# Modulation products grouped by four beside the long convolutions of a two-layer trunk

## The chip, the cores and the metric

The kernel runs on one core of one Trainium2 chip. Its engines work through queues of their own, in the order of their instructions, and wait for each other by semaphores: TensorE (PE, with its weight loads listed as PEld), VectorE (DVE), ScalarE (ACT), GpSimd (POOL) and SyncE (SP), whose queue issues nearly all the loads and stores of this kernel. The metric is the time of one execution on the device in microseconds (us); lower is better.

## The reference

Two layers of a diffusion trunk run over 1024 latent rows and 128 context rows of width 1024. Each layer first forms a modulation vector from the two condition vectors (one for the latents, one for the context), then mixes the rows by four head groups (latent attention, windowed attention, a gated delta recurrence, a long convolution), and then applies an MLP. The change concerns the first line only:

```python
mod = silu(cond) @ w_ada + b_ada              # w_ada is 1024 x 6144 for each layer
sh1, sc1, gt1, sh2, sc2, gt2 = split(mod, 6)
h = rms_norm(x, g_pre_mix) * (1.0 + sc1) + sh1
o = mixer(h)                  # attention, windowed attention, recurrence, convolution
x = x + gt1 * rms_norm(o, g_post_mix)
h = rms_norm(x, g_pre_mlp) * (1.0 + sc2) + sh2
x = x + gt2 * rms_norm(square(relu(h @ mlp_w1)) @ mlp_w2, g_post_mlp)
```

All inputs are float32. `w_ada` is 24 MB for a layer, read once.

## The kernel before

The Python code is a program of generators. `run_timed` runs several of them side by side in the order of planned times, and a scheduler of the tile framework then sets the order of the instructions on each engine from dependences and its own planned times. What stands in that order is fixed when the program is built; on the chip every engine keeps to it.

The six parts of the modulation are made in three pieces of 2048 columns, by `ada(l, g)` (L385): `g` is 0, 1 or 2. Piece 0 of layer 0 stands at the start of the program (the lead). Three generators run side by side in `layer` (L2134): `rest()` (the projections, then `hyena`, then `attention`), `other()` (the filters and preparation of the recurrence, then `gdn_scan`) and `adas()`, which waits until `rest()` says "proj" and then makes pieces 1 and 2 of its own layer and, in layer 0, piece 0 of layer 1.

In `ada`, the 1024 rows of the weights are eight steps `kt` of 128 rows. In each step four tiles `wada` of 128 x 512 (256 KB) are loaded by SP, and each has one product: the 128 x 32 slice `cst[:, kt]` of the conditions is the stationary side, the weights stream through, and the result is added in the rows 32h to 32h + 31 of one PSUM tile `ada` (h is 0 to 3). So a piece is 32 loads and 32 products, and each product is recorded as two passes (two weight loads and two matmuls). ACT then copies the tile to `adarow`, PE transposes it to `adat`, and DVE adds the bias into `mod`. All `wada` tiles come from the pool "T", which has four buffers, so the fifth load waits for the first product. The pool "L" has eight buffers and holds the weights of the projections. A product stands where the scheduler has put it, alone or beside others.

The names that the steps of the prediction use, in the order of a layer:

- `pj`: the products of the input projections.
- `u`, `dS`, `St`, `sdec`, `sc`, `Q`: the gated delta recurrence, `gdn_scan`. A step reads the state `St` on PE (24 small products `u<-St`), forms `u` on DVE, multiplies on PE again (`dS`, `u<-u`), and DVE updates the state (`St<-sdec,dS`, twice in a step). The next step needs this state. One scan has 16 steps over the latents and 2 over the context.
- `long_conv` runs twice in `hyena`: DVE and POOL make a length-12 transform (`ZA`, `ZB`, `ZC`), PE the forward transforms (`X`), DVE and POOL the products with the filters (`pw`, `Y`; the filter `Hs` is loaded by SP), PE the way back (`iz`), and DVE some 25 additions (`pmx`, `e`, `f`, `y`). At the end DVE multiplies `y` by the rows `x` that SP has loaded from `uscr`.
- `hoT`: the transposes of the convolution's result. `oT`: those of the recurrence's result.
- `S`: the scores of head 0's preparation, with the row maxima `mx` on DVE (`ahead()` in `hyena`, 24 of each). `mT`, `mrow`, `mscr`: the maxima are transposed, written to DRAM and read back as one row of `Q`, after which the first tile `ST` of the attention can run.
- `ST`, `e`, `eh`, `el`, `O`: the attention, one head after another, beside the `S` of the next head.

## Time and profile before

| | us |
|---|---|
| median of 3 runs | 3829.02 |
| the three runs | 3819.71, 3829.02, 3829.53 |
| the profiled execution, its time | 3828.84 |
| the profiled execution, its span | 3827.1 |
| layer 0: last `pj` to first `ST` | 535 to 724 |
| layer 0: attention | 724 to 1020.5 |
| layer 1: last `pj` to first `ST` | 2440 to 2636 |
| layer 1: attention | 2636 to 2902 |

The places of a stage are read from the timeline. A window's row gives the busy time of each engine within it, so that a stretch in which PE is busy nearly all the time can be told from one in which it waits. The granted clock in the same row says at which of its two levels (0.5 is 1.2 GHz, 1.0 is 2.4 GHz) TensorE ran, as a mean over the window.

### The profile page before, as it was taken

The page shows a single profiled execution, that of the slowest core. Times are in us where ns is not written, and L with a number is a line of the kernel's source. Part 1 is how long each engine was busy: PE and PEld are TensorE (multiplying, and loading weights), DVE is VectorE, ACT ScalarE, POOL GpSimd, SP SyncE. Part 2 cuts the span into 40 slices and gives each one's busy share as a digit, 9 for nine tenths or more (in the row PEclk, how much of TensorE's full clock was granted, in tenths as well). Part 3 has the DMA queues.
Part 4 walks back from the last instruction along what each step waited for, and adds up shares of the span by engine and source line. Part 5 has one row for each costly group of instructions (what it writes and reads, how often), then busy time and mean ns, then how long its engine had stood idle before and what let it go on. Part 6 is the DMA issues. An engine that isn't in the chain of part 4 may idle for free. (4 is left out here: it accounts for less than half of the span.)

```text
span 3827.1 us, 57478 instructions
## 1 busy us (share of the span) xinstructions
PE 3531.1 (92%) x21710; PEld 2958.8 (77%) x21710; DVE 2279.6 (60%) x4583; ACT 1355.6 (35%) x2970; POOL 853.1 (22%) x806
## 2 busy tenths in 40 slices
PE   7989888899899999999989798787999999999998
PEld 4879764366689999999968797645666899999997
DVE  5765577696645444444586664768884544444446
ACT  5434343264542222122354234323564422222112
POOL 1151521264430000000131524213553200000003
PEclk9999889897899999999999898897889999999999
DMA  5356486831421111111234465756314211111113
GB/s 202 115 120 158 139 275 202 235 90 39 138 87 47 45 44 34 44 45 45 96 103 131 108 144 161 258 187 177 84 50 138 72 45 45 45 45 42 40 41 121
DMA packets 364672, 405.31 MB, mean 106 GB/s; under 512 B 115815, under 2 KB 237157, under 8 KB 364394
## 3 DMA queue, kind: packets, MB, share of 16 engines
q1 hardware_dynamic: 364394, 401.63, 34.9%
q8 instruction: 171, 2.80, 0.3%
q14 instruction: 107, 0.88, 0.1%
HBM read 298.34 MB, written 103.19 MB: 105 GB/s over the span
## 5 line engine op out<-in xcount | busy, mean ns | idle before, releaser
L213 PE MATMUL hid<-hT,w1h 128*128 128x384 f32 x3072 | 786.5, 335 | 0.1
L213 PE MATMUL pj<-hT,wah 128*128 128x384 f32 x2112 | 575.1, 351 | 9.0 <-ACT wah L253 4.2
L1831 DVE TENSOR_TENSOR acc<-acc,mo 128x512 f32<-128x512 f32 x504 | 346.1, 687 | 391.8 <-PE mo L213 391.8
L213 PEld LDWEIGHTS hid<-hT,w1h 128*128 128x128 f32 x3072 | 557.7, 188 | 14.4 <-ACT h L481 1.1
L213 PE MATMUL hid<-hT,w1l 128*128 128x384 f32 x1536 | 514.1, 335 | 0.0
L213 PE MATMUL mo<-w2h,ul 128*128 128x512 f32 x1116 | 435.0, 392 | 0.0
L213 PE MATMUL mo<-w2h,uh 128*128 128x512 f32 x1080 | 422.7, 391 | 0.0
L213 PE MATMUL mo<-w2l,uh 128*128 128x512 f32 x1080 | 422.7, 391 | 0.0
L213 PEld LDWEIGHTS pj<-hT,wah 128*128 128x128 f32 x2112 | 395.3, 196 | 21.9 <-issue 7.8
L662 POOL TENSOR_TENSOR e<-e,e 128x512 f32<-128x512 f32 (+1 forms) x216 | 307.3, 1424 | 313.8 <-DVE el L232 145.2
L269 POOL TENSOR_TENSOR postr<-postr,mhalf 128x1 f32<-128x1 f32 x36 | 22.3, 621 | 1568.9 <-DVE postr L268 1568.6
L213 PE MATMUL pj<-hT,wal 128*128 128x384 f32 x1056 | 367.5, 348 | 0.7 <-DVE wal L232 0.7
L242 ACT CAST w2h<-w 128x512 fp32r<-128x512 f32 x128 | 70.3, 619 | 732.9 <-PE mo L213 728.8
L213 PEld LDWEIGHTS hid<-hT,w1l 128*128 128x128 f32 x1536 | 288.3, 188 | 2.5
L232 DVE TENSOR_TENSOR el<-e,eh 128x512 fp32r<-128x512 f32 (+1 forms) x252 | 241.4, 977 | 25.1 <-ACT eh L653 20.4
L213 PEld LDWEIGHTS mo<-w2h,ul 128*128 128x128 f32 x1116 | 209.6, 188 | 46.1
L213 PEld LDWEIGHTS mo<-w2h,uh 128*128 128x128 f32 x1080 | 202.8, 188 | 37.5
L213 PEld LDWEIGHTS mo<-w2l,uh 128*128 128x128 f32 x1080 | 202.7, 188 | 36.5
L213 PEld LDWEIGHTS pj<-hT,wal 128*128 128x128 f32 x1056 | 206.3, 195 | 4.6 <-issue 2.0
L1814 DVE SCALAR_TENSOR_TENSOR relu<-hid,relu 128x384 f32<-128x384 f32 x180 | 99.5, 554 | 166.9 <-ACT relu L1813 166.9
L213 PE MATMUL ada<-wada,cst 128*32 128x512 f32 x384 | 130.8, 692 | 45.5 <-DMA wada<-in_w_ada 45.4
L232 DVE TENSOR_TENSOR wal<-wa,wah 128x512 fp32r<-128x512 f32 x88 | 67.6, 773 | 147.2 <-ACT wah L253 118.2
(502 smaller groups left out, 6366.6 us busy)
## 6 DMA issues: line engine op xcount, KB each, us to landing
w<-in_w SPq DMA_DIRECT2D x256, 256.0 KB
wada<-in_w_ada SPq DMA_DIRECT2D x192, 256.0 KB
wa<-in_wa SPq DMA_DIRECT2D x88, 256.0 KB
x<-xres SPq DMA_DIRECT2D x21, 512.0 KB
x<-in_x SPq DMA_DIRECT2D x18, 512.0 KB
Q<-rscr SPq DMA_DIRECT2D x32, 288.0 KB
o<-oscr SPq DMA_DIRECT2D x18, 512.0 KB
xres<-x SPq DMA_DIRECT2D x36, 256.0 KB
```

The lines of the kernel that those rows point to most:

```text
L213: self.last = self.nc.tensor.matmul(out, l, r, start=start, stop=stop, skip_group_check=True)
L232: self.nc.vector.tensor_tensor(out=lo, in0=x, in1=hi.bitcast(F32), op=ALU.subtract)
L242: self.nc.scalar.copy(out=hi[:, q], in_=st)
L269: self.nc.gpsimd.tensor_tensor(out=out, in0=out, in1=self.bcs(self.mhalf[:out.shape[0]], out.shape), op=ALU.pow)
L662: self.nc.gpsimd.tensor_tensor(out=acc, in0=acc, in1=e, op=ALU.add)
L1814: nc.vector.scalar_tensor_tensor(out=r[:, :n], in0=ps[:, :n], scalar=0.0, in1=r[:, :n], op0=ALU.max, op1=ALU.mult)
L1831: nc.vector.tensor_tensor(out=acc[t][:, ns], in0=acc[t][:, ns], in1=ps, op=ALU.add)
```

## The change

`ada` loads the four tiles of a step together and issues their products as a group: the product of h = 3 is placed behind the last product that stood in the program, and the three others behind it. The products of a step are issued when the loads of two later steps have been issued (`len(wait) == 3`), except in the lead, where they follow at once. Two steps in three take their tiles from the pool "L" (eight buffers), the third from "T" (four). `hyena` says "conv" when it has issued its loads, and `adas()` waits for "conv" instead of "proj". In `attention`, `self.heads` is set: from there on all tiles come from "T", and a step's products follow before the loads of the next step. `layer` sets it back.

```diff
--- before.py
+++ after.py
@@ -382,17 +382,37 @@
         nc.scalar.copy(out=kr[0:32], in_=st[0:32])
         nc.sync.dma_start(out=self.krow.rearrange("o (p c) -> (o p) c", p=32), in_=kr[0:32, 0:44].bitcast(F32))
 
-    def ada(self, l, g, tag="T"):
+    def ada(self, l, g, tag=""):
+
 
         nc = self.nc
         ps = self.P(name="ada")
+        wait = []
+
+        def products(after):
+            kt, w = wait.pop(0)
+            with self.tc.issue_after(after.ins) if after else contextlib.nullcontext():
+                self.mm(ps[96:128, :], self.cst[:, kt], w[3], kt == 0, kt == 7)
+                with self.tc.issue_after(self.last.ins):
+                    for h in range(3):
+                        self.mm(ps[32 * h:32 * h + 32, :], self.cst[:, kt], w[h], kt == 0, kt == 7)
         for kt in range(8):
+            while wait and self.heads:
+                products(self.last)
+            names = tag or ("TTTT" if self.heads or kt % 3 == 2 else "LLLL")
+            w = [self.H(name="wada", tag=names[h]) for h in range(4)]
             for h in range(4):
-                w = self.H(name="wada", tag=tag[h % len(tag)])
-                i = nc.sync.dma_start(out=w, in_=self.I["w_ada"][l, kt, :, g * 2048 + h * 512:g * 2048 + (h + 1) * 512])
-                self.mm(ps[32 * h:32 * h + 32, :], self.cst[:, kt], w, kt == 0, kt == 7)
+                i = nc.sync.dma_start(out=w[h], in_=self.I["w_ada"][l, kt, :, g * 2048 + h * 512:g * 2048 + (h + 1) * 512])
             if l == g == 0:
                 self.lead = i
+            wait.append((kt, w))
+            if tag:
+                products(None)
+            elif len(wait) == 3:
+                products(self.last)
+            yield
+        while wait:
+            products(self.last)
             yield
         row = self.H(name="adarow")
         nc.scalar.copy(out=row, in_=ps)
@@ -1014,6 +1034,7 @@
 
         sk = self.sinks(l)
         self.pend = []
+        self.heads = True
 
         def swa(g):
             if g == 0:
@@ -1711,6 +1732,7 @@
         fwdp, invp = (fi[:, a:b].rearrange("p (c f) -> p c f", c=2) for a, b in ((0, 194), (194, 450)))
         nc.sync.dma_start(out=fwdp, in_=self.I["fwdp"])
         nc.sync.dma_start(out=invp, in_=self.I["invp"])
+        self.done.add("conv")
         yield HY
         for o in range(2):
             conv = self.long_conv(l, o, cur, fwd, inv, ahead)
@@ -2092,13 +2114,14 @@
             with self.tc.issue_after(self.lead.ins):
                 self.late_consts()
         self.done = set()
+        self.heads = False
 
         def until(x):
             while x not in self.done:
                 yield 1
 
         def adas():
-            yield from until("proj")
+            yield from until("conv")
             for a in ((l, 1), (l, 2)) + (((l + 1, 0),) if l + 1 < DEPTH else ()):
                 for _ in self.ada(*a):
                     yield 5
```

PE has as many instructions as before. Their order is the same outside the lead, the stage from the last `pj` to the first `ST` of each layer, and the attention of layer 0.

PE, layer 0, around the first forward transform `X` of the first convolution. Before:

```order
L213 MATMUL u_5413<-u_5430,Q_3515 64x64
L213 MATMUL u_5413<-u_5430,Q_3557 64x64
L213 MATMUL dS_5435<-u_5430,sc_5040 64x64 x2
L213 MATMUL dS_5435<-u_5430,kt_4891 64x64 x2
L213 MATMUL dS_5441<-u_5430,sc_5040 64x64 x2
L213 MATMUL dS_5441<-u_5430,kt_4893 64x64 x2
L213 MATMUL X_6594<-ZA_6476,fwd_6290 128x256 x2
L213 MATMUL X_6606<-ZA_6476,fwd_6294 128x256 x2
L213 MATMUL X_6617<-ZA_6476,fwd_6292 128x256 x4
L213 MATMUL u_5478<-St_754_4897,sc_5403 64x64
```

After, the last products of a step of the recurrence, a group of the modulation (`ada`), and the same `X`:

```order
L213 MATMUL u_6403<-u_6420,sc_6262 64x64 x2
L213 MATMUL u_6403<-u_6420,Q_3515 64x64
L213 MATMUL u_6403<-u_6420,Q_3557 64x64
L213 MATMUL ada_6314<-wada_6318,cst 32x512
L213 MATMUL ada_6314<-wada_6315,cst 32x512
L213 MATMUL ada_6314<-wada_6316,cst 32x512
L213 MATMUL ada_6314<-wada_6317,cst 32x512
L213 MATMUL X_6586<-ZA_6468,fwd_6290 128x256 x2
```

Counted by its reads of the state (`u<-St`), one step of the recurrence stood between the last `pj` and these `X`, seven beside the first convolution, three beside the second and two behind it. Now ten stand before `X`, three beside the first convolution and none behind that. In layer 1 it was one, six and three; now it is six, four and none. The first group of the modulation comes right before `X`.

PE, layer 0, the scores `S` of head 0 and the transposes `hoT` of the convolution's result. Before:

```order
L213 MATMUL S_7475<-K_7307,Q_7305 128x384
L213 MATMUL S_7478<-K_7307,Q_7305 128x384
L213 MATMUL S_7481<-K_7307,Q_7305 128x384
L213 MATMUL S_7481<-Q_7305 128x128
L229 MATMUL hoT_7485<-ident,y_1170_7301 128x128 x4
L229 MATMUL hoT_7493<-ident,y_1171_7302 128x128 x4
L229 MATMUL hoT_7501<-ident,pz_7231 128x128
L213 MATMUL ada_7506<-wada_7507,cst 32x512
L213 MATMUL ada_7506<-wada_7510,cst 32x512
```

After, from the middle of the 24 `S`:

```order
L213 MATMUL S_7402<-K_7275,Q_7273 128x384
L213 MATMUL S_7402<-Q_7273 128x128
L213 MATMUL S_7406<-K_7275,Q_7273 128x384
L213 MATMUL S_7409<-K_7275,Q_7273 128x384
L213 MATMUL ada_7090<-wada_7323,cst 32x512
L213 MATMUL ada_7090<-wada_7320,cst 32x512
L213 MATMUL ada_7090<-wada_7321,cst 32x512
L213 MATMUL ada_7090<-wada_7322,cst 32x512
L213 MATMUL S_7412<-K_7275,Q_7273 128x384
L213 MATMUL S_7412<-Q_7273 128x128
```

Before, the 24 `S` stood behind the last products of piece 2 and right before `hoT`. Now they stand between its groups: one group before the second convolution's last stretch (`iz`), three behind it, one in the middle of `S`, and three between `S` and `hoT`.

PE, layer 0, the start of head 0's attention (`ST`, `O`), with piece 0 of layer 1. Before:

```order
L213 MATMUL S_7692<-Q_7579 128x128
L213 MATMUL S_7709<-K_7581,Q_7579 128x384
L213 MATMUL ada_7506<-wada_7564,cst 32x512
L213 MATMUL ST_7712<-Q_7305,K_7307 128x512
L213 MATMUL ST_7712<-Q_7306,K_7307 128x512
L213 MATMUL ST_7712<-Q_7305,K_7308 128x512
L213 MATMUL ST_7744<-Q_7305,K_7307 128x512
L213 MATMUL ST_7744<-Q_7306,K_7307 128x512
L213 MATMUL ST_7744<-Q_7305,K_7308 128x512
L213 MATMUL O_7648<-eh_7655,VA_7309 128x512
L213 MATMUL ada_7506<-wada_7567,cst 32x512
L213 MATMUL S_7725<-K_7581,Q_7579 128x384
```

After:

```order
L213 MATMUL ST_7597<-Q_7274,K_7275 128x512
L213 MATMUL ST_7597<-Q_7273,K_7276 128x512
L213 MATMUL ada_7553<-wada_7557,cst 32x512
L213 MATMUL ada_7553<-wada_7554,cst 32x512
L213 MATMUL ada_7553<-wada_7555,cst 32x512
L213 MATMUL ada_7553<-wada_7556,cst 32x512
L213 MATMUL ST_7624<-Q_7273,K_7275 128x512
L213 MATMUL ST_7624<-Q_7274,K_7275 128x512
L213 MATMUL ST_7624<-Q_7273,K_7276 128x512
L213 MATMUL ST_7644<-Q_7273,K_7275 128x512
L213 MATMUL ST_7644<-Q_7274,K_7275 128x512
L213 MATMUL ST_7644<-Q_7273,K_7276 128x512
```

The products that stood one by one among `ST`, `S` and `O` stand in eight groups of four, spread over the heads 0 and 1.

## Rows read from the trace of the kernel before

**Rows 1.** The page's costliest groups: busy us, mean ns | idle before it, its releaser.

```profile
L213 PE MATMUL ada<-wada,cst 128*32 128x512 f32 x384 | 130.8, 692 | 45.5 <-DMA wada<-in_w_ada 45.4
```

**Rows 2.** By stretch: us; PE, PEld, DVE, ACT, POOL busy (instructions); clock, DMA share, GB/s.

```profile
535.00:549.00 14.00, 5.44 (x75) 2.96 (x75) 13.45 (x32) 6.92 (x22) 6.26 (x5) 0.50 1.02 344
549.00:614.00 65.00, 57.82 (x556) 32.87 (x556) 45.98 (x157) 19.10 (x67) 9.91 (x15) 0.94 0.79 273
614.00:657.00 43.00, 38.41 (x364) 25.36 (x364) 34.62 (x108) 13.41 (x50) 14.30 (x17) 1.00 0.58 178
657.00:724.00 67.00, 43.91 (x280) 22.03 (x279) 45.16 (x133) 14.59 (x42) 5.24 (x2) 0.72 0.84 248
2440.00:2456.00 16.00, 4.77 (x75) 3.05 (x74) 15.75 (x32) 4.85 (x16) 7.58 (x5) 0.63 1.00 360
2456.00:2528.00 72.00, 62.67 (x534) 34.95 (x527) 46.58 (x158) 21.08 (x73) 9.81 (x14) 0.87 0.71 242
2528.00:2574.00 46.00, 42.85 (x364) 26.62 (x368) 34.78 (x109) 13.64 (x49) 14.81 (x17) 0.93 0.55 171
2574.00:2636.00 62.00, 35.06 (x153) 21.72 (x153) 49.40 (x121) 7.87 (x18) 5.22 (x2) 0.69 0.85 249
724.00:1020.50 296.50, 272.68 (x1192) 177.54 (x1192) 221.04 (x357) 161.21 (x324) 153.53 (x108) 0.87 0.34 88
2636.00:2902.00 266.00, 245.12 (x1126) 172.27 (x1127) 217.41 (x338) 160.75 (x323) 153.72 (x108) 0.86 0.27 68
```

**Rows 3.** The same view of the modulation's products alone, on PE.

```profile
0.00:40.00 40.00, 19.00 (x64) 1.00 0.83 295
549.00:614.00 65.00, 20.71 (x64) 0.94 0.79 273
614.00:657.00 43.00, 8.18 (x36) 1.00 0.58 178
690.00:780.00 90.00, 28.58 (x64) 0.87 0.74 210
2456.00:2528.00 72.00, 22.51 (x64) 0.87 0.71 242
2528.00:2574.00 46.00, 11.30 (x36) 0.93 0.55 171
```

**Rows 4.** Waits between 2430 and 2620 us: us in total, times, longest.

```profile
PE ada L213 <- DMA wada<-in_w_ada: 27.9, 7, 14.5
```

**Rows 5.** Timeline of PE: start, duration, operation, records; two records are one product.

```profile
645.80 1.07 PE L213 MATMUL ada<-wada,cst 128*32 128x512 f32 x8
742.20 1.05 PE L213 MATMUL ada<-wada,cst 128*32 128x512 f32 x2
```

**Rows 6.** Timeline: recurrence steps, DVE's state updates and PE's reads of the state.

```profile
537.23 0.27 DVE L1368 TENSOR_TENSOR St<-sdec,dS 128x128 f32<-128x128 f32 x1
545.29 0.29 DVE L1368 TENSOR_TENSOR St<-sdec,dS 128x128 f32<-128x128 f32 x1
655.00 0.34 PE L213 MATMUL u<-St,sc 64*64 64x64 f32 x8
655.28 0.41 PE L213 MATMUL u<-St,qT 64*64 64x64 f32 x16
659.17 0.27 PE L213 MATMUL u<-St,sc 64*64 64x64 f32 x1
```

**Rows 7.** Timeline, layer 0: from the second convolution's end to the first attention tile.

```profile
682.17 1.23 DVE L1726 TENSOR_TENSOR y<-y,x 128x1024 f32<-128x1024 f32 x1 [3.78 <-DMA x<-uscr]
686.91 9.24 DVE L767 TENSOR_REDUCE mx<-S 128x1 f32<-128x384 f32 x18
705.55 0.42 PE L229 MATMUL mT<-ident,nm 128*8 128x128 f32 x1
724.19 1.20 PE L213 MATMUL ST<-Q,K 97*128 97x512 f32 x4
```

**Rows 8.** Timeline, layer 0's attention: SP's queue.

```profile
737.91 18.52 SPq L392 DMA_DIRECT2D wada<-in_w_ada  x13
```

## The prediction

> **What bounds the kernel now.** I read the page first. It has one group for the modulation's products [rows 1]: 384 records, 130.8 us of PE, and 45.5 us in which PE stood idle for their weights. Against a span of 3827.1 us that is at most 4.6%, so this change can move little, and only where these 176 us lie on the path. I then cut the two stages and the two attentions into stretches [rows 2], because a mean over the program mixes places with different limits. In both convolutions PE is busy 87 to 93% of the time and DVE 65 to 81%: PE is the first bound there, DVE a close second. Before the first convolution (535 to 549, 2440 to 2456) DVE is busy 96 and 98%, PE under 40%, and the DMA engines are full. Behind the second convolution neither is full: 44 and 45 of 67 us in layer 0, 35 and 49 of 62 in layer 1; that is a chain of latencies. Attention is PE's in both layers, 92% busy; yet layer 0's is 30.5 us longer than layer 1's with nearly the same DVE time (221 against 217 us) and 27.6 us more of PE, and the modulation, which layer 1's attention does not have, is there with 28.58 us [rows 2, 3].
>
> **What a product costs alone and in a group.** Four products side by side, eight records, took 1.07 us; one product alone, two records, took 1.05 [rows 5]. The four go to different columns of the array and run at the same time, so four that stand apart cost four times as much. A piece has eight steps; in groups it is 8 x 1.07 = 8.6 us where PE runs at its full clock. The lead is left out of the sum: PE has 19.00 us of products in 40 us there while the DMA engines are 83% busy [rows 3], so what grouping frees is hidden under the loads; without that cover it would be the 10 us by which 19.00 exceeds 8.6, a gain.
>
> **Layer 0's attention.** Piece 0 of layer 1 takes 28.58 us of PE [rows 3] and will take 8.6. That is 20 us of an engine which is 92% busy, so I count 20/0.92 = 21.7 and round to 21. A check from the other side: the attention of layer 1, without a piece, is 30.5 us shorter [rows 2], and 8.6 of that stays. The queue of SP speaks for some loss: before, its stretch from 737.91 on issued 13 loads one behind the other's product and took 18.52 us [rows 8]. Now 16 loads stand there in one piece, and behind them the write of the next maxima (`mscr`), which the next head's first `ST` waits for. They are one head ahead of need, so I charge nothing; if that cover is gone it costs at most those 18.52 us, and the term falls to 2.
>
> **The stage of layer 0, stretch by stretch.** *Before the first `X`*: nine recurrence steps more stand there. The cleanest lone step in the trace reads the state at 655.00 and again at 659.17, 4.2 us [rows 6]. That holds one modulation burst in it, so it is not flattered. From above there is the step from 537.23 to 545.29, 8.1 us, in which DVE also did the rotations and the first transform [rows 6, 2]. From below, DVE alone needs 14 instructions of at most 0.27 us, which I take as 3. DVE's old work of this stretch (13.45 us) fits partly into the gaps of the lone steps, so I take 3.7: 9 x 3.7 = +33 us. *First convolution*: PE loses four steps (1.4 us each, twice the 0.69 us from 655.00 to the end of the burst of reads) and 20.71 us of products, and gets four groups back; four more lie in the pause before the second convolution. 57.82 - 5.6 - 20.71 + 4.3 = 36 us of PE; DVE loses four steps, 45.98 - 12 = 34. With PE filled to 78% and DVE to 74%, less than either reaches as the busier engine of a stretch now, it is 46 us where it was 65: -19. *Second convolution*: PE falls from 38.41 by 8.18 and three steps to about 28. But DVE loses three steps (9 us) and takes over the normalisation of the recurrence's result, which came later and is about as much. It keeps its 35 of 43 us and becomes the bound; at 87% of it the stretch is 40 us: -3. *Behind it*: the 24 maxima move ahead of the multiplication by `x`. They take 24/18 of 9.24 us, 12.3 [rows 7], and lay bare on the path between that multiplication (682.17) and `hoT`; with the steps and the normalisation gone as well I count -15. What stays is the chain from `mT` to `ST`, 18.6 us [rows 7]. Sum for layer 0: 33 - 19 - 3 - 15 = -4 us.
>
> **The load of `x` is moved past work.** SP now issues the first `x` of the second convolution behind a load that waits for a group in the middle of the 24 `S`. Before, DVE already waited 3.78 us for `x` [rows 7]. The wait can grow, but the maxima are at hand to fill it. I charge nothing; uncovered it is one load more, some 4 us in each layer.
>
> **The stage of layer 1.** The same steps with its own rows. *Before `X`*: five steps more, 5 x 3.7 = +18. *First convolution*: PE 62.67 - 22.51 + 6.4 (six groups) - 2.8 = 44 us, DVE 46.58 - 6 = 41; at 81 and 76% some 54 us where it was 72: -18. The waits for weights, 27.9 us between 2430 and 2620 [rows 4], are in part within it. *Second*: PE to 28, DVE stays near 35 of 46: -5. *Behind*: as in layer 0, -15; here the long waits for weights stood beside DVE's normalisation, so I count no more for them. Sum: 18 - 18 - 5 - 15 = -20 us.
>
> **The sum.** -4 - 20 - 21 = -45 us on the profiled execution's 3828.84 us, whose span is 3827.1; it stands 0.18 us under the median of the three runs (3829.02). That makes 3784 us. The MLPs, the projections and layer 1's attention keep their order and their time.
>
> **A rule that speaks against it.** TensorE's granted clock follows how busy PE has been: it is 0.50 and 0.63 in the two stretches before the first `X`, where PE is busy 39 and 30%, and 0.94 to 1.00 in layer 0's convolutions, where it is busy 89% [rows 2]. The change makes the first kind of stretch longer (ten and six lone steps) and thins out PE in the second. If the clock stays at its lower level, 1.2 GHz, through all lone steps and the first half of each convolution, the lone steps pay their 1.4 us of PE twice, 16 x 1.4 = 22 us, and the convolutions keep their old speed at worst for some 10 us. The Trainium skill says the same in "TensorE: Matmul & The Clock Gate", section "HAM oscillation — how this bites in real kernels": a PE that waits between short bursts falls back to half its clock and starts the next burst cold. The trace agrees with it in the stretches named. The lone step of rows 6 stands in a convolution, where PE ran at full clock, so this price is not in my sum.
>
> **The rivals.**
> *Clock.* The 22 to 32 us just worked out come back: 3784 + 28 = 3812 us. For it: the rows of the stretches before `X`. Against it: in a lone step DVE and ACT have longer parts than PE, and part of PE's slower passes lies beside them.
> *DVE keeps the stage.* DVE has 139 us of the 189 in layer 0's stage and 147 of 196 in layer 1's (sums of rows 2), and not one of its instructions goes away. If it is filled no better than before, the stages stay as they are (layer 0's even pays some us for the lone steps), and only the attention gains: 3829 - 21 + 10 = 3818 us, which is hardly told from no change.
> *Lone steps at full price: slower.* Each of the 14 steps that are moved before `X` (nine and five) costs the 8.1 us of the step at 537.23 rather than 3.7, because the loads of its operands and the stores of its results share full DMA engines with the convolution's tables and the first weights. 14 x 4.4 = 62 us, 3784 + 62 = 3846 us. It decides from 45/14 = 3.2 us more a step, 6.9 us a step. For it: the DMA share of 1.00 and 1.02 and DVE's 96% in just these stretches. Against it: DVE's work there is not repeated for each step, and the step at 655 shows what is left.
> *Deeper.* PE's waits for weights and all of the freed time come off the path and DVE fills to 90%: stages of 155 and 163 us, -34 and -33, with the attention's -21 some -88: 3741 us. Against it: lone steps leave DVE idle by construction.
> That the change does not do what it says, products of a group one after the other, is excluded by rows 5 as long as all four tiles have landed.
>
> **How the numbers follow.** Forecast (3770 to 3800 us): 0.45. Deeper than that: 0.17. Clock, 3800 to 3817 us: 0.14. DVE keeps the stage, within 0.3% of the median (3817.5 to 3840.5, about what a measurement of this kernel can tell from no change): 0.13. Lone steps at full price: 0.11. So faster by over 0.3% has 0.45 + 0.17 + 0.14 = 0.76, the same 0.13, slower 0.11. The range from 3748 to 3828 us leaves out the slower rival, half of the "same" and the far end of "deeper".
>
> **What would show it.** In the profile after: the modulation's group with 384 records and some 50 to 60 us busy instead of 130.8, and its wait for weights mostly gone; layer 0's attention near 275 us, its 28.58 us of products near 9; the stages near 185 and 176 us, with the time before the first `X` at 45 to 50 us in layer 0 and 30 to 36 in layer 1; state updates 3.5 to 4.5 us apart there. The forecast is wrong if they are 7 us or more apart, if DVE waits long for `x` or `Hs` behind modulation loads in SP's queue, or if the clock in the convolutions drops under 0.8.

## The result, and the profile after

The changed kernel is slower: a median of 3880.33 us (3867.1 to 3890.2, four runs) against 3824.36 us for the kernel before (3818.2 to 3829.53, four runs); the ratio is 1.0138 [1.0114, 1.0162]. The prediction was 3784 us. Its range and its sign were wrong. The rival that it gave 0.11, the lone recurrence steps, came nearest, with a second loss beside it that no rival had named. Medians are of runs in the ordinary, fast state; that of e1 leaves out one execution of 11318.66 us.

Both profiled executions, cut at the same marks in the program (us):

| stretch | before | after | difference | predicted |
|---|---|---|---|---|
| start to layer 0's last projection `pj` | 535.8 | 527.6 | -8.2 | 0 |
| layer 0: `pj` to the first `X` | 13.1 | 76.1 | **+63.0** | +33 |
| first `X` to the second convolution's `X` | 70.8 | 57.5 | -13.3 | -19 |
| to the end of the second `iz` | 37.5 | 40.6 | +3.1 | -3 |
| to the first `ST` | 67.0 | 47.4 | -19.6 | -15 |
| layer 0: `ST` to the MLP (`hid`) | 399.9 | 410.3 | **+10.4** | -21 |
| `hid` to layer 1's last `pj` | 1316.4 | 1316.5 | 0 | 0 |
| layer 1: `pj` to the first `X` | 15.7 | 53.7 | **+38.0** | +18 |
| first `X` to the second convolution's `X` | 78.1 | 57.9 | -20.2 | -18 |
| to the end of the second `iz` | 39.7 | 37.5 | -2.2 | -5 |
| to the first `ST` | 62.4 | 48.6 | -13.8 | -15 |
| layer 1: `ST` to the end | 1190.6 | 1205.7 | +15.1 | 0 |
| span | 3827.1 | 3879.4 | +52.4 | -45 |

The marks lie within some us of the windows of [rows 2], not on them. The modulation's group, which answers to [rows 1], does what was forecast of it:

```profile
L213 PE MATMUL ada<-wada,cst 128*32 128x512 f32 x384 | 67.2, 808 | 21.2 <-DMA wada<-in_w_ada 21.2
```

PE's busy time in it falls from 130.8 to 67.2 us and its wait for weights from 45.5 to 21.2. So 88 us less of PE's time went to the modulation, and the program is 52 us longer. By stretch (us; PE, PEld, DVE, ACT, POOL busy; clock, DMA share, GB/s), to be laid beside [rows 2]:

```profile
528.00:560.00 32.00, 11.07 (x224) 9.47 (x224) 25.77 (x82) 12.55 (x40) 8.77 (x5) 0.55 1.00 360
527.60:603.70 76.10, 34.68 (x681) 28.83 (x681) 46.13 (x184) 37.63 (x131) 8.77 (x5) 0.52 0.56 193
603.70:661.20 57.50, 38.51 (x360) 26.17 (x357) 43.22 (x126) 14.22 (x43) 19.67 (x19) 0.83 0.67 226
2476.00:2529.70 53.70, 20.75 (x393) 16.47 (x393) 35.35 (x121) 24.70 (x81) 9.91 (x6) 0.54 0.75 261
2529.70:2587.60 57.90, 43.77 (x488) 29.41 (x484) 46.98 (x144) 18.56 (x65) 17.47 (x18) 0.85 0.63 201
749.20:953.70 204.50, 188.31 (x802) 120.64 (x802) 154.50 (x242) 104.61 (x199) 108.26 (x73) 0.84 0.38 101
569.56:601.71 32.15, 18.55 (x387) 16.46 (x384) 16.67 (x85) 20.05 (x72) 0.00 (x0) 0.50 0.16 47
```

The rows from 527.60 and from 2476.00 are the two stretches before the first `X`. PE is busy 46 and 39% of them, DVE 61 and 66%, ACT 49 and 46%: no engine is full. In layer 0 the DMA engines are full up to 560 (first row, share 1.00), and in the second half (last row) they are nearly idle too, at 0.16. There it is a chain in which each engine waits for the one before it. DVE's state updates (timeline: start, duration, engine, line, operation, records, wait before it) show its beat:

```profile
535.22 0.27 DVE L1389 TENSOR_TENSOR St<-sdec,dS 128x128 f32<-128x128 f32 x1
547.67 0.47 DVE L1389 TENSOR_TENSOR St<-sdec,dS 128x128 f32<-128x128 f32 x2
...
569.56 0.47 DVE L1389 TENSOR_TENSOR St<-sdec,dS 128x128 f32<-128x128 f32 x2
580.27 0.47 DVE L1389 TENSOR_TENSOR St<-sdec,dS 128x128 f32<-128x128 f32 x2
...
601.71 0.47 DVE L1389 TENSOR_TENSOR St<-sdec,dS 128x128 f32<-128x128 f32 x2
```

From 569.56 to 601.71 six steps pass, 32.15 us, 5.36 us each. In one step DVE works 16.67/6 = 2.8 us, PE 3.1 and ACT 3.3; put one behind the other that would be 9.2, so the three overlap in part, and no engine's own time sets the step. The four intervals before them, 535.22 to 569.56, are slower: 8.6 us each, and 12.5 us from 535.22 to 547.67. The waits of this stretch (528 to 603; us in all, times, longest):

```profile
PE dS L213 <- DVE u L1383: 16.4, 9, 3.5
PE u L213 <- DVE St L1389: 10.7, 6, 3.4
DVE sc L1402 <- ACT sc L1401: 10.0, 10, 1.2
PE u L213 <- DMA sc<-sscr: 6.1, 1, 6.1
```

The first three are the hand-overs: PE waits for DVE's `u` and for its state, DVE for ACT's copy out of PSUM. The fourth is a load of the step's operands. Three windows of the slow part (columns as above) and SP's queue show what stands beside it:

```profile
535.22:547.67 12.45, 3.08 (x62) 2.52 (x62) 11.10 (x30) 4.99 (x17) 6.55 (x4) 0.50 1.05 374
554.24:559.51 5.27, 3.11 (x60) 2.58 (x59) 2.60 (x15) 3.53 (x12) 0.00 (x0) 0.50 0.99 370
560.00:563.65 3.65, 0.17 (x3) 0.00 (x0) 1.60 (x9) 3.00 (x11) 0.00 (x0) 0.50 0.09 29
560.88 2.67 SPq L1405 DMA_DIRECT2D goscr<-sc  x2
563.65 0.85 SPq L1349 DMA_DIRECT2D sc<-sscr  x2
```

In the slowest interval DVE is busy 11.10 of 12.45 us, most of it with the rotations and the first transform. From 554.24 to 559.51 the DMA engines are just as full (0.99), and the step's first update comes after 5.3 us, as in the steady chain. The load that PE waits 6.1 us for was issued only at 563.65, behind a store of the recurrence's results in SP's queue; the DMA share was 0.09 until then. So full DMA engines stand beside the slow start, but the trace does not show that they are its cause.

In layer 0's attention PE's time for the third piece did fall, from 28.58 us [rows 3] to 11.89 (the modulation's products on PE alone: us, busy, clock, DMA share, GB/s):

```profile
749.20:850.00 100.80, 11.89 (x64) 0.86 0.38 112
```

and yet the attention is longer. The timeline of ACT shows where it stops:

```profile
782.48 0.60 ACT L671 ACTIVATE e<-ST 128x512 f32<-128x512 f32 x1 [0.45 <-DVE el L232]
783.11 0.62 ACT L673 CAST eh<-e 128x512 fp32r<-128x512 f32 x1
809.73 0.59 ACT L418 COPY adarow<-ada 128x512 f32<-128x512 f32 x1 [26.00 <-PE ada L213]
812.81 0.60 ACT L671 ACTIVATE e<-ST 128x512 f32<-128x512 f32 x1 [2.49 <-PE ST L213]
```

The copy of the piece's result out of PSUM (`adarow`) stands in ACT's queue in front of the next exponentials. ACT waits 26.00 us for the piece's last group; `ST` and `O` have no exponentials to go on with, and PE has neither of them from 786.9 to 811.1. PE's groups of the piece, and SP's loads of its weights, tell why the last one is late:

```profile
750.65 1.94 PE L213 MATMUL ada<-wada,cst 128*32 128x512 f32 x8
758.13 1.06 PE L213 MATMUL ada<-wada,cst 128*32 128x512 f32 x8 [0.16 <-DMA wada<-in_w_ada]
...
807.65 1.94 PE L213 MATMUL ada<-wada,cst 128*32 128x512 f32 x8 [3.36 <-DMA wada<-in_w_ada]
752.60 23.49 SPq L405 DMA_DIRECT2D wada<-in_w_ada  x16
```

The groups come about 8 us apart (eight from 750.65 to 807.65). All four tiles of a group come from the pool "T" of four buffers, so the next loads can start only when the group has read them, and each group waits for a whole load. The piece was done 37 us behind the first `ST` before (761.4); now it takes 60 (809.6).

### The profile page after: what moved, and what is told of

Its sections match the earlier page's. It is cut to its first block, busy times and chain, and to the rows that moved or that the text cites. A ratio compares the mean times of both kernels' runs of the same rounds, so it can differ in the third digit from the quotient of the medians.

```text
span 3879.4 us, 57492 instructions
## 1 busy us (share of the span) xinstructions
PE 3510.8 (90%) x21710; PEld 2978.2 (77%) x21710; DVE 2291.7 (59%) x4583; ACT 1359.2 (35%) x2968; POOL 857.0 (22%) x806
## 5 line engine op out<-in xcount | busy, mean ns | idle before, releaser
L213 PEld LDWEIGHTS hid<-hT,w1h 128*128 128x128 f32 x3072 | 557.6, 188 | 14.5 <-ACT h L501 1.1
L232 DVE TENSOR_TENSOR el<-e,eh 128x512 fp32r<-128x512 f32 (+1 forms) x252 | 249.5, 1012 | 29.5 <-ACT eh L673 26.8
L213 PEld LDWEIGHTS mo<-w2h,uh 128*128 128x128 f32 x1080 | 202.8, 188 | 37.5
L213 PEld LDWEIGHTS pj<-hT,wal 128*128 128x128 f32 x1056 | 206.8, 196 | 3.3 <-issue 1.7
L1835 ACT ACTIVATE relu<-hid 128x384 f32<-128x384 f32 x180 | 87.8, 488 | 184.6 <-PE hid L213 184.6
```

Source lines behind the costliest of these rows:

```text
L213: self.last = self.nc.tensor.matmul(out, l, r, start=start, stop=stop, skip_group_check=True)
L232: self.nc.vector.tensor_tensor(out=lo, in0=x, in1=hi.bitcast(F32), op=ALU.subtract)
L1835: nc.scalar.activation(out=r[:, :n], in_=ps[:, :n], func=AF.Relu)
```

## The experiments

The letters of the theories are those of the expectations. **A**: the link by which each group is placed behind the last product of the program (`issue_after(self.last.ins)`, called the outer link below) pushes lone recurrence steps in front of the first `X`. **C**: the early copy `adarow` on ACT costs the attention its gap. **G**: the clock of 0.50 makes a lone step dear; **H**, against it: the chain of hand-overs does, whatever the clock. **K**: the links cost time wherever a group stands, not only before `X`.

An edit moves more than its own instructions, because the scheduler plans everything behind it anew: e3, which touches the copy alone, has two more reads of the state before layer 1's first `X` than the changed kernel. And the stretches are those of one profiled execution of each kernel, which for e2, e3, e6, e8 and e9 was the slowest of its runs; the medians and ratios are the firmer evidence.

Stretches of the profiled executions (us, layer 0 / layer 1; "stage" is `pj` to `ST`, "heads" the first `ST` to the last `O` of the full-attention heads), with the ratio to the kernel before:

| kernel | `pj` to first `X` | stage | heads | ratio |
|---|---|---|---|---|
| before | 13.1 / 15.7 | 188.4 / 195.9 | 202.4 / 175.9 | 1 |
| changed | 76.1 / 53.7 | 221.6 / 197.7 | 204.5 / 178.3 | 1.0138 [1.0114, 1.0162] |
| e1 no link | 17.5 / 19.0 | 192.0 / 190.0 | 207.6 / 191.2 | 1.0054 [1.0031, 1.0077] |
| e2 first group free | 15.0 / 23.5 | 212.3 / 213.1 | 196.8 / 182.4 | 1.0073 [1.0046, 1.01] |
| e3 late copy | 75.8 / 62.6 | 219.4 / 201.8 | 180.6 / 183.2 | 1.0053 [1.0029, 1.0078] |
| e4 no link, late copy | 16.6 / 21.1 | 191.8 / 186.5 | 195.2 / 179.7 | 0.9978 [0.9959, 0.9997] |
| e5 before, late copy | 14.5 / 21.4 | 189.3 / 190.6 | 191.6 / 188.6 | 1.0019 [1.0001, 1.0038] |
| e7 busy steps (one run) | 63.6 / 58.2 | 206.8 / 209.2 | 202.5 / 170.9 | 1 run |
| e8 an eighth of the work | 24.0 / 31.8 | 184.0 / 181.3 | 186.6 / 197.0 | 0.9928 [0.9906, 0.9949] |
| e9 later start | 17.8 / 18.1 | 214.4 / 201.8 | 189.5 / 182.3 | 1.0078 [1.0056, 1.0101] |
| e12 as e4, again | 16.1 / 19.7 | 190.5 / 182.1 | 188.8 / 182.7 | 0.9965 [0.9949, 0.9981] |

**e1: the outer link taken away.**

```diff
-            with self.tc.issue_after(after.ins) if after else contextlib.nullcontext():
+            with contextlib.nullcontext():
```

> The changed kernel without the outer link of a group to the last product of the program (the three products stay linked to the fourth). The recurrence steps that stood alone before the first forward transform go back: one (layer 0) and two (layer 1) instead of ten and six. Theory A (the link holds the first transform behind lone steps, and these cost 63 and 38 us): about 3880 - 101 plus some 35 us that the convolutions give back, 3815 us, first transform 13 to 16 us after the last projection. Theory B (the stage is set by VectorE or by loads, the place of the steps is indifferent): 3880 us, the 101 us turn up beside the convolutions.

Measured: 3847.11 us, ratio 1.0054. The time before `X` is back at 17.5 and 19.0 us, and the stages give back 29.6 and 7.7 us of the changed kernel's. So the link does place the lone steps (A). But the time is 0.54% above the kernel before, some 20 us, and 32 us above the 3815 us of A, so the link is not the whole loss.

**e2: the link taken from the first group of piece 1 alone.**

```diff
-            with self.tc.issue_after(after.ins) if after else contextlib.nullcontext():
+            with self.tc.issue_after(after.ins) if after and (kt or g != 1) else contextlib.nullcontext():
```

> The changed kernel, with the outer link taken from one group alone in each layer, the first one (piece 1, step 0). One and five steps stand before the first transform instead of ten and six; the later groups keep their links. Theory A: nearly all of what the full removal brings in layer 0, about 3830 to 3840 us. Theory B: 3880 us.

Measured: 3845.98 us, ratio 1.0073. Before `X` there are 15.0 us in layer 0, and the stage is still 212.3 (in an execution of 3869.85 us, 24 over the median). The steps went elsewhere, into the pause between the convolutions, which grew from 24.2 to 65.3 us (us; PE, PEld, DVE, ACT, POOL busy; clock, DMA share, GB/s):

```profile
589.20:654.50 65.30, 31.75 (x571) 21.02 (x571) 42.85 (x162) 27.22 (x97) 4.53 (x3) 0.66 0.41 134
```

This too is a stretch in which no engine is busy over 66%. Some eight steps stand in it, with seven groups of the modulation. So steps are dear in other places than before `X` too.

**e3: the third piece's copy put off to head 3.** The piece's generator waits for "late", which the loop over the heads sets at its fourth head.

```diff
+        if getattr(self, "heads", False):
+            while "late" not in self.done:
+                yield
         row = self.H(name="adarow")
-        nc.scalar.copy(out=row, in_=ps)
+        with self.tc.issue_after(self.last.ins) if getattr(self, "heads", False) else contextlib.nullcontext():
+            nc.scalar.copy(out=row, in_=ps)
...
         for i in range(6):
+            if i == 3:
+                self.done.add("late")
```

> The changed kernel, with ScalarE's copy of the third piece (piece 0 of layer 1) put off until head 3 of layer 0's attention. Theory C (the copy stands in ScalarE's queue ahead of head 1's exponentials and waits 26 us there for the last group): layer 0's gap of 24.2 us in the attention products goes, 3880 - 20 = 3860 us. Theory D (the attention is held by the loads of the piece on SyncE's queue, whatever the copy does): 3880 us, the gap stays.

Measured: 3843.21 us, ratio 1.0053. The copy no longer waits (ACT's timeline of this kernel):

```profile
857.32 0.59 ACT L422 COPY adarow<-ada 128x512 f32<-128x512 f32 x1
```

and the heads of layer 0 take 180.6 us where they took 204.5: 23.9 us, about the 24.2 us (786.9 to 811.1) in which `ST` and `O` stood still in the changed kernel. No gap of them is longer than 5.3 us now, so the gap was the copy's (C). The granted clock of the heads is also higher, 0.91 against 0.84, and C had forecast a gain of 20 us; by the ratios it is 33.

**e4: both edits, e1's and e3's.**

> Both edits: no outer link, and the copy of the third piece put off. If theories A and C hold and add up: 3815 - 20 = 3795 us, faster than the kernel before. If only A holds: 3815. If neither: 3880.

Measured: 3811.61 us, ratio 0.9978. The four kernels make a square. By the ratios, taking away the link is worth 0.84% with the early copy and 0.75% with the late one (32 and 29 us), and putting off the copy 0.85% with the link and 0.76% without it (33 and 29 us), each with an interval of some 12 us to either side (worked out from those of the ratios). So the two losses add up within the noise, their sum of 61 us is more than the whole slowdown of 53, and what is left without them is a gain of some 0.2 to 0.4% (e4, e12). That 3811.61 lies near the 3815 us expected "if only A holds" is chance: e1 shows that the link alone gives 3847.

That the copy's gap explains its 29 to 33 us is shown for one side of the square only. ACT's copy in the kernel before, and in e1:

```profile
761.44 0.58 ACT L398 COPY adarow<-ada 128x512 f32<-128x512 f32 x1 [21.96 <-PE ada L213]
778.46 0.58 ACT L418 COPY adarow<-ada 128x512 f32<-128x512 f32 x1 [9.94 <-PE ada L213]
```

Without the link the copy waited 9.94 us and `ST` and `O` stood still for 7.8 us around it; yet putting it off was worth as much. The heads of layer 0 got 12.3 us shorter in e4 and 18.8 in e12. Where the rest comes from stays open.

**e5: the kernel before with the late copy alone.**

```diff
+        if l != self.lay:
+            while "late" not in self.done:
+                yield
         row = self.H(name="adarow")
-        nc.scalar.copy(out=row, in_=ps)
+        with self.tc.issue_after(self.last.ins) if l != self.lay else contextlib.nullcontext():
+            nc.scalar.copy(out=row, in_=ps)
```

> The kernel before, with only the copy of the third piece put off until head 3; products stay single, all tiles from pool T. Theory E (grouping gives the gain of the run with no outer link and the late copy, 0.9978): no gain here or less than 5 us, 3822 us. Theory F (the late copy alone gives it, since the kernel before had a 17.5 us gap of the same kind, and grouping gives nothing that shows): 3805 to 3812 us.

Measured: 3836.37 us, ratio 1.0019 [1.0001, 1.0038]. ACT waited 21.96 us for this copy in the kernel before as well, and `ST` and `O` stood still for 17.5 us. The heads of layer 0 do get 10.8 us shorter, but the rest of the attention gets 8.5 longer, at a clock of 0.87 instead of 0.92, and layer 1 behind its first `ST` 23.8, which the edit does not touch but whose order the scheduler has changed too. Moving the copy is no gain in itself: the view that the early copy costs any kernel its gap falls, and F with it. The length of the gap does not tell the worth of the edit: 17.5 us and no gain here, 24.2 and 33 in e3, 7.8 and 29 in e4.

**e6: no link, late copy, but the products right behind their loads and all tiles from "T".** This takes the early loads out of e4.

```diff
-            names = tag or ("TTTT" if self.heads or kt % 3 == 2 else "LLLL")
+            names = tag or ("TTTT")
...
-            elif len(wait) == 3:
+            elif True:
                 products(self.last)
```

> No outer link and the late copy, and the weights no longer loaded two steps ahead: groups of four at once behind their loads, all tiles from pool T (four buffers) as in the kernel before. If the early loads matter: some 10 us over the run with them (3812), 3822 us. If only the grouping matters: 3812 us.

Measured: 3834.81 us, ratio 1.0021 [0.9997, 1.0045], against 0.9978 and 0.9965 for e4 and e12. The stages are 203.9 and 195.2 us long. Grouping without the early loads and the buffers of "L" gains nothing that was measured. Whether the early loads would bring the gain without grouping was not run.

**e7: the changed kernel, with eight products of 128 columns more in each recurrence step.** They feed nothing; they only keep PE busy, so that the clock rises.

```diff
-            pu = [self.P((2, 3, 64), "u", "Q") for _ in range(2)]
+            full = [self.P((512,), "u", "Q") for _ in range(2)]
+            pu = [f[:, 0:384].rearrange("p (a b c) -> p a b c", a=2, b=3) for f in full]
...
+            for j in range(8):
+                self.mm(full[j % 2][:, 384:512], self.ident, self.ident, True, True)
```

> The changed kernel with eight products of 128 columns more in each recurrence step (their result is used by nobody), placed where TensorE waits for VectorE's u. Nine and seven steps stand alone before the first transform. Theory G (a lone step takes 5.3 us because TensorE is at its lower clock there): the granted clock rises over 0.8 in the lone stretch and a step takes 4.2 to 4.5 us. Theory H (the step is a chain of hand-overs between four engines and the clock has little part in it): 5.3 us or more whatever the clock.

Measured in one run: 3865.95 us. The stretch of lone steps (window, then two of eight updates on DVE), and the added products of one step on PE with what follows them:

```profile
570.40:605.39 34.99, 27.00 (x570) 24.29 (x570) 18.89 (x99) 23.28 (x85) 0.00 (x0) 1.00 0.23 71
570.40 0.48 DVE L1392 TENSOR_TENSOR St<-sdec,dS 128x128 f32<-128x128 f32 x2 [0.60 <-PE dS L213]
...
605.39 0.47 DVE L1392 TENSOR_TENSOR St<-sdec,dS 128x128 f32<-128x128 f32 x2
576.50 2.05 PE L213 MATMUL u<-ident 128*128 128x128 f32 x16
579.50 0.27 PE L213 MATMUL dS<-u,sc 64*64 64x64 f32 x2 [0.95 <-DVE u L1386]
```

The clock is now 1.00, and seven steps take 34.99 us, 5.0 each, where they took 5.36 at 0.50. The added products do not hide a larger worth of the clock: they end at 578.55, and PE then waits 0.95 us more for DVE's `u`. So a lone step stays near 5 us at either of the two levels, 1.2 and 2.4 GHz. G, which wanted 4.2 to 4.5 us, falls; H holds but for the 0.36 us. The Trainium skill, in "TensorE: Matmul & The Clock Gate", section "HAM oscillation — how this bites in real kernels", says that a PE with waits between short bursts drops to half its clock. The trace agrees on the drop (0.50 to 0.54 before `X`). The low clock costs this chain little, because DVE's `u` waits less for PE's reads of the state than for the additions before it in DVE's own queue (the lines are under "Why the prediction was wrong").

**e8: the kernel before with one of the eight steps in each piece but the lead.** Seven eighths of those pieces' loads and products are left out, so this was meant as a bound on what any better placing of them can gain, not as a variant of the kernel.

```diff
-        for kt in range(8):
+        kts = range(8) if l == g == 0 else (7,)
+        for kt in kts:
```

> The kernel before, with one of the eight steps in each piece but the lead: seven eighths of these sums, loads and products left out. The bound of what any better placing of the modulation could bring. Theory I (the modulation lies on the path in both stages and in layer 0's attention): some 60 to 70 us less, 3760 us. Theory J (most of it is hidden beside the recurrence and the chain of the stage): 20 to 30 us less, 3800 us, nearly all in the attention.

Measured: 3799.01 us, ratio 0.9928 [0.9906, 0.9949]: some 28 us under the kernel before. Heads and the rest of layer 0's attention take 384.0 us instead of 399.9 together, the stages 4.4 and 14.6 us less: 35 us in the places for which the prediction had summed 45. The total is not a strict bound. In the profiled execution layer 1 behind its first `ST`, where none of this work stands, is 37.5 us longer; its heads ran at a clock of 0.76 instead of 0.84, and what lies between them and the MLP at 0.86 instead of 0.96. By how much that lengthens the median run is not known.

**e9: the changed kernel, its pieces started one step of the first convolution later.**

```diff
-        self.done.add("conv")
...
             for i, t in enumerate(conv):
+                if i == 0:
+                    self.done.add("conv")
```

> The changed kernel with all its links, its pieces started one step of the generator later: the signal for them comes when the first convolution's length-12 transform has been issued, not when its loads have been. The first group then stands behind the first forward transforms, and one and two steps of the recurrence stand alone before these. Theory A (it is the lone steps ahead of the first transform that cost, not the links as such): about 3835 to 3845 us, as with the link of the first group taken away (3846). Theory K (a link to the last product anywhere makes its place serial): 3865 us or more.

Measured: 3858.78 us, ratio 1.0078. Before `X` it is 17.8 and 18.1 us, yet the stages are 214.4 and 201.8: with the links in place the second convolution is now held up, 67.0 us from its `X` to the end of `iz` in layer 0 (37.5 before) and 56.9 in layer 1 (39.7). In layer 0 five steps read the state there, where three did before and none in the changed kernel:

```profile
608.50:675.50 67.00, 51.04 (x488) 34.19 (x492) 37.80 (x132) 22.58 (x72) 16.35 (x17) 0.79 0.53 173
```

The time lies between the two forecasts, nearer to K's: with the links, the place of the damage follows the place of the groups. That they take the scheduler's freedom to put steps and groups where PE would wait anyway fits this, but is argued.

**e10 and e11: e9 with the late copy, and e9 with the late copy and without the link.** The edits are those of e9, e3 and e1.

> The same later start, and the copy of the third piece put off; its groups stand among the heads 2 and 3. If the two gains add: 3840 - 35 = 3805 us. If the third piece only moves its wait to later heads: 3830 us.

> The later start, no outer link, and the late copy. The bound with seven eighths of the pieces left out was 0.9928 of the kernel before, 3797 us. If the late start takes the modulation off the first convolution without a price: 3800 to 3805 us; if the start of the pieces was no limit any more: 3812 us as without it.

Measured: e10 3838.99 us, 1.002 [1.0006, 1.0034], with stages of 221.1 and 207.5 us; e11 3818.84 us, 0.9976 [0.9961, 0.9991], with 190.7 and 196.8. Neither forecast of e10 came: with its piece among later heads, the copy waits 13.09 us at 935.98, behind the heads. e11 is 7 us over the higher of its two. The link costs 20 us here. A later start is no better than an early one without links.

**e12: e4's kernel once more.**

> The kernel without outer link and with the late copy again, in five rounds, for its interval: 0.9978 of the kernel before if the first measurement was right; 1.000 if its gain was noise.

Measured: 3811.27 us, 0.9965 [0.9949, 0.9981]. It is faster than both kernels, than the one before by 0.35%. Its modulation's group and the beginning of its stage of layer 0, to be laid beside those of before and after:

```profile
L213 PE MATMUL ada<-wada,cst 128*32 128x512 f32 x384 | 70.8, 750 | 16.1 <-DMA wada<-in_w_ada 15.9
532.40:548.50 16.10, 5.61 (x105) 3.94 (x105) 14.71 (x40) 6.80 (x20) 7.24 (x5) 0.71 1.01 346
548.50:616.70 68.20, 50.85 (x582) 34.85 (x580) 53.37 (x172) 23.13 (x82) 14.31 (x17) 0.85 0.80 279
```

The modulation's products on PE alone, in the second of these stretches, and in the like stretch of the kernel before under it:

```profile
548.50:616.70 68.20, 9.12 (x56) 0.85 0.80 279
548.90:619.70 70.80, 21.76 (x68) 0.95 0.74 256
```

With the steps back beside the convolutions, the first convolution with the pause behind it is 68.2 us long (70.8 before), though PE has 12.6 us less of these products in it. Half of that became idle time of PE (17 us of the stretch instead of 11), some 4 us went to PE's other products at the lower clock (0.85 instead of 0.95), and 2.6 us made the stretch shorter.

## Why the prediction was wrong

**The first step that failed is the price of a lone step.** In layer 0 nine updates more do stand before `X`; in layer 1 five, or six with one at the very edge of the stretch. The 3.7 us were wrong: a step cost 63.0/9 = 7.0 us in layer 0 and 38.0/5 = 7.6 in layer 1 (6.3 with the sixth), 7.2 on the mean of the 14, over the 6.9 from which the rival decided. Of this 5.36 is the steady chain of layer 0; the rest goes with the slow start, in which DVE had other work and PE waited 6.1 us for a load that SP issued late. The two terms before `X` were too small by 30 and 20 us.

Two things misled. The step of [rows 6] was read from PE's read of the state at 655.00 to the next one at 659.17. But the state read at 655.00 had been updated at 650.13; from update to update (658.82) that step took 8.7 us. In the time before the late read, ACT and DVE had already done what stands between an update and `u` in a lone step. The kernel before first, then a lone step of the changed kernel:

```profile
650.13 0.47 DVE L1368 TENSOR_TENSOR St<-sdec,dS 128x128 f32<-128x128 f32 x2
653.25 0.51 ACT L1380 ACTIVATE Q<-u,eo 64x64 f32<-64x64 f32 x2
655.74 0.22 DVE L1362 TENSOR_TENSOR u<-u,sc 128x64 f32<-128x64 f32 x1 [0.28 <-PE u L213]
581.20 0.73 PE L213 MATMUL u<-St,qT 64*64 64x64 f32 x15
582.80 0.56 DVE L1402 TENSOR_TENSOR Q<-Q,u 64x64 f32<-64x64 f32 x2
583.39 0.22 DVE L1383 TENSOR_TENSOR u<-u,sc 128x64 f32<-128x64 f32 x1
```

Before, `u` starts at once when PE's reads are done. In the lone step PE's reads end at 581.93, but `u` starts at 583.39, right behind the additions that DVE does with ACT's copies. This part was missing from the 4.2 us. And the lower bound added up DVE's instructions alone (3 us), although PE, DVE and ACT hand the step to each other and their parts overlap only in part. The rival (8.1 us) was nearer in the price, but its reason, full DMA engines, is not what the trace shows: the step beside a DMA share of 0.99 was no slower than the steady ones.

**The second is layer 0's attention.** PE's 28.58 us did become 11.89, as the first half of the term said. The conversion, 20/0.92, failed: it holds only if nothing but PE sets the pace. ACT's wait for `adarow` was in the trace of before (21.96 us), the products that it waits for are the ones that the change regroups, and the prediction did not ask when the last of them would be done. It also charged nothing for the "T" pool's four buffers, named SP's 18.52 us as the worst case [rows 8], and read the bound off SP's queue rather than off the buffers: a group every 8 us. The term is +10.4 instead of -21. Of this the heads are +2.1; of the 8.3 behind them 7.9 lie in the windowed attention (last section). That putting off the copy is worth 33 us, more than the 24.2 us of its gap, is measured and not explained.

**The convolutions and what is behind them** were right in sign, and near in size: -29.8 against -37 in layer 0, -36.2 against -38 in layer 1. But e1 and e12 show that this is no gain of its own: where the steps come back beside the convolutions, the stages are within 4 us of before in layer 0 and 6 to 14 us shorter in layer 1. The gain was mostly the same steps, moved. For layer 0 without the links the rival "DVE keeps the stage" is thus near the mark in its result: the stage stays as it was while PE is relieved. DVE has 53.37 of 68.2 us of the first convolution there, 78%, and it was not tried whether that is what holds it.

**The sum.** Beside these, the start to the last projection was counted at nothing and gained 8.2 us; layer 1 behind its first `ST` was counted at nothing and lost 15.1, with 5.3 of it in the windowed attention and 7.3 in the output projection. The prediction's reason for the nothing was that the order there stays the same. It does not: in the trace PE's `ST`, `S` and `O` follow each other differently, and of ACT's four short `mes` of the windowed attention, which stood together before (first line), the last now stands behind another copy:

```profile
2822.09 0.85 ACT L858 ACTIVATE mes<-nm,sink 128x1 f32<-128x1 f32 x4
2862.23 0.65 ACT L878 ACTIVATE mes<-nm,sink 128x1 f32<-128x1 f32 x3
2862.91 0.58 ACT L738 COPY oh<-sO 64x512 f32<-64x512 f32 x1
```

The clock between the heads and the MLP is lower as well, 0.93 instead of 0.96. No run tells the two apart. From the MLP (`hid`) to the end, where the order is the same, layer 1 takes 815.5 us in both. Term by term, +30, +20, +31.4, +7.2, +1.8, -8.2 and +15.1 lead from -45 to the measured +52.4.

**The other rivals.** *Clock*: the clock is low before `X`, at 0.52 and 0.54, but e7 shows that it is worth 0.36 us of a step. In the convolutions of layer 0 it did fall, from 0.95 and 1.00 to 0.83 and 0.84, above the 0.8 that the text had set as the mark; what that cost there no run tells. *Deeper* wanted stages of 155 and 163 us; e8, with seven eighths of the pieces' work gone, has 184.0 and 181.3, and a time that is lower by 28 us, not 88. Of the signs for a wrong forecast, updates "7 us or more apart" came in layer 1 (8.6 on the mean of six) and nearly in layer 0 (6.6 on the mean of ten).

## What to carry to other kernels

A step that is handed from engine to engine cost its whole latency here wherever little stood beside it, so price a moved step by the period of a chain, from one update to the next, in a stretch with nothing else in it, and by the sum of its hand-overs when there is no such stretch. An interval that begins with a late read leaves out what the other engines did meanwhile. Grouping paid here only when the groups were free of the link: an order that was pinned to the last product of the program took about 30 us, more than the grouping gave. And when the producer of a value is moved, look up who waits for it in an in-order queue: putting off one copy in front of other work on ACT was worth about 30 us in both pairs of kernels, though nothing in the kernel before.

## What the runs showed that was not expected

The same kernel can run one stretch at different clocks in two executions. This is the windowed attention of layer 0 in e4 and in e12, one kernel, and the same stretch before and after (us; PE, PEld, DVE, ACT, POOL busy; clock, DMA share, GB/s; in this order):

```profile
915.90:1022.00 106.10, 93.40 (x418) 65.53 (x418) 71.05 (x116) 58.99 (x127) 44.72 (x36) 0.72 0.18 52
911.60:1006.00 94.40, 79.36 (x418) 55.12 (x418) 72.86 (x117) 58.36 (x128) 46.65 (x36) 0.86 0.23 66
926.60:1021.00 94.40, 81.55 (x414) 56.85 (x414) 69.41 (x116) 57.87 (x127) 46.63 (x36) 0.83 0.22 62
953.70:1056.00 102.30, 87.08 (x398) 60.23 (x397) 68.63 (x103) 58.42 (x126) 44.16 (x35) 0.75 0.21 58
```

The work is alike (418 PE records), and the stretch takes 106.1 us at a granted clock of 0.72 and 94.4 at 0.86. So the 7.9 us by which the changed kernel's profiled execution is longer there (102.3 against 94.4) may be its clock of 0.75 in this execution, and cannot be put down to the change alone. Of the lone steps the opposite was unexpected: twice the clock gave a chain of small products 0.36 us of 5.36.
